# Multiplying the reciprocal norm in where the first stage modulates its rows, straight from PSUM

## The chip, the core and the metric

One core of a Trainium2 chip runs the whole program. The metric is device time in microseconds of one execution; for the kernel before, three runs gave 1878.0, 1878.12 and 1881.57 us, so the median is 1878.12 us.

## What is computed

Two layers of a diffusion backbone run over 512 latent tokens and 256 context tokens, with 1024 channels. The change touches only the start of the first layer, where every token is normalized, scaled and shifted before the input projections:

```python
def rmsnorm(x, w):
    y = xf * lax.rsqrt(jnp.mean(xf * xf, axis=-1, keepdims=True) + EPS)
    return y * w
def modulate(h, shift, scale):
    return h * (1 + scale) + shift
mod   = split(c_act  @ mod_w[layer] + mod_b[layer], 6)
mod_c = split(cc_act @ mod_w[layer] + mod_b[layer], 6)
hx = modulate(rmsnorm(x, norm_mix_w[layer]), mod[0], mod[1])
hc = modulate(rmsnorm(h_ctx, norm_mix_w[layer]), mod_c[0], mod_c[1])
```

The projections `hx @ ab_w_in` and `hc @ ab_w_in` follow, then the DeltaNet and attention heads, the output projection, the feed-forward network, and a second layer with other heads.

## The kernel before, in words

Activations lie with the channels on the partitions: `xt` is 8 blocks of 128 channels by 768 tokens (512 latent, 256 context). Every large product is done in three passes: each operand is split into a high part in a rounded format (`hi`, `wh`) and a low part with the rest (`lo`, `wl`), and TensorE adds `wh*hi`, `wh*lo` and `wl*hi`. A split is one ScalarE copy (L247 for weights, L405 for activations) and one subtraction (L197, by VectorE, or by GpSimd for every other activation block).

The first stage is in `body`, L1692 to L1712. `norm_stats` (L368) sums the squares of the 8 blocks, gets the reciprocal norm of each token, and lets TensorE spread it over all partitions into two PSUM tiles with the tag `mm`: one for the 512 latent tokens, one for the 256 context tokens. Then L1701 to L1703 multiply `xt` by them in place, with two VectorE instructions for each of the 8 blocks, 16 in all.

The loop at L1706 runs four times. Step i calls `mod` (L312), which loads 2 MB of modulation weights in two transfers, multiplies on TensorE (64 short matmuls), copies the result out of PSUM (L328), transposes it (L194) and adds the bias (`modc`). `scale_shift` makes the scales (`samix`). `hx0` (L394) then modulates the channel blocks 2i and 2i+1: two VectorE `tensor_scalar` instructions for each block (L403, recorded as L214), which write a tile `hxt` (three buffers), then the split (L405, L406). At i = 1 `dn_begin` (L690) takes the first two weights of the convolution projections, and for each of them two PSUM tiles of the tag `mm`; `dn_part` (L693) then adds channel blocks 0 and 1 at step 1, 2 and 3 at step 2, and 4 and 5 at step 3, for both weights: 6 matmuls of 384 columns for each block and weight. Blocks 6 and 7 are added in `dn_conv` (L697). Its ScalarE copies (L712) empty the PSUM tiles, and the third weight follows.

The tag `mm` has four PSUM buffers (L1695). In the kernel before, the two norm tiles have been read for the last time when the 16 multiplications are done, so that all four are there for the two begun weights. The queues run in an order fixed when the program is built: a planner places each engine's instructions by the program's order, by when their inputs are ready in its model, and by when a buffer is free; an instruction whose tile has no free buffer yet is placed behind the release. All transfers of this stage are issued in order on SP's queue (L221).

The stage for the later norms, `hx` (L408), already has the form that the change brings in: VectorE multiplies a block by its scale and by the norm from PSUM in one instruction (L420), and ScalarE adds the shift (L424).

Of the kernel before, what the change touches and what calls it, by code (L numbers as in the profile page):

```python
# [13 lines left out]
AF = mybir.ActivationFunctionType  # L14
ALU = mybir.AluOpType
# [6 lines left out]
KD = D // P  # L22
NL = 512
NC = 256
NT = NL + NC
# [123 lines left out]
class Kern:  # L149
# [241 lines left out]
            K.mm(o, rs[:, i:i + 1].broadcast_to([P, P]), K.ident)  # L391
        return pl, pc

    def hx0(self, xt, act, sa, sb, d0):  # L394
        K = self
        if d0 % 4 == 0:
            for a in act:
                x = K.t(K.bp, (P, 4, NT), "hx", F32R, bufs=4)
                a.extend(x[:, d] for d in range(4))
        for d in range(2):  # L400
            t = K.t(K.sx, (P, NT), "hxt", bufs=3)
            for c, g in ((slice(0, NL), 0), (slice(NL, NT), 1)):
                K.ts(t[:, c], xt[:, d0 + d, c], sa[:, d, g:g + 1], sb[:, d, g:g + 1])  # L403
            hi, lo = act[0][d0 + d], act[1][d0 + d]
            K.A.copy(out=hi, in_=t)  # L405
            K.sub(lo, t, hi, K.G if d % 2 else K.V)  # L406

# [1271 lines left out]
def body(ctx, tc, I, out, dbg=None, stop=None):  # L1679
    K = Kern(ctx, tc, I, out, dbg)  # L1680
    K.setup()
    hD = K.t(K.dp, [2, 2, P, 2, 2, 512], "hD")
    hsD = K.t(K.dp, [2, 4, P, 2, 512], "hsD")
    sg, sp = ExitStack(), ExitStack()
    K.pg = K.pool(sg, "dn_g", side="right")
    mp0 = K.pool(sp, "mp0", side="right")
    half = lambda w, ns: [(w[n][i], (4, 256)) for n in ns for i in range(2)]
    outp = lambda w, n: [(w[n][dp], (2, 4, P)) for dp in range(4)]
    K.stream([(I["abf"][n], (KD, P)) for n in (4, 5, 6, 7, 0, 1, 2, 3)] + [(I["abg"], (KD, P))]
             + [(I["abf"][n], (KD, P)) for n in (8, 9, 10, 11)] + half(I["abt"], (4, 5, 2, 3, 0, 1))  # L1690
             + outp(I["abo"], 1) + outp(I["abo"], 0))
    with ExitStack() as s:  # L1692
        with ExitStack() as s2:
            K.mp, K.mpn = K.pool(s2, "mps"), 6
            K.psum(mm=4, wk=4)  # L1695
            K.sp = K.sx = K.pool(s2, "sp0", side="right")
            xt = K.t(K.bp, (P, KD, NT), "x", bufs=1)
            for d in range(0, KD, 2):
                K.dma(xt[:, d:d + 2], I["xall"][:, d:d + 2])
            st = K.norm_stats(xt)  # L1700
            for d in range(KD):  # L1701
                for c, r in ((slice(0, NL), st[0]), (slice(NL, NT), st[1][:, :NC])):
                    K.mul(xt[:, d, c], xt[:, d, c], r)  # L1703
            act = ([], [])
            begun = []
            for i in range(4):  # L1706
                K.mod(i)
                K.hx0(xt, act, *K.scale_shift(0, "mix", 2 * i, 2), 2 * i)
                if i == 1:
                    begun = [K.dn_begin() for _ in range(2)]  # L1710
                for b in begun:
                    K.dn_part(b, act, range(2 * i - 2, 2 * i))  # L1712
        K.mp, K.mpn = mp0, 1
        pf = K.pool(s, "hyf0")
        K.tasks["hy"] = [K.hy_time(pf, hsD)]
        K.tasks["mod"] = [K.mod_gen(range(4, 10))]
        conv = K.l0_conv(act, sg, sp, begun)
        K.drain("hy")
    od, x1D, oh = K.l0_mixers(act, conv)
    if stop == "mix0":  # L1720
        for k in range(KD):
            h = K.t(K.cp, (P, NT), "dbh", bufs=1)
            o = od if k < 4 else oh
            K.tt(h, o[0][:, k % 4], o[1][:, k % 4], ALU.add)
            K.dma(dbg["o"][k], h)
        return
    xt = K.t(K.bp, (P, KD, NT), "x", bufs=1)
    for d in range(KD):
        K.dma(xt[:, d], x1D[:, d])
    K.out_half(None, 0, od, xt, None, NT)  # L1730
    saf, sbf = K.scale_shift(0, "ffn")
    with ExitStack() as s:
        K.sp = K.sx = K.pool(s, "sp1", side="right")
        pf = [K.pool(s, "hyf1a"), K.pool(s, "hyf1b", side="right")]
        act = K.hx(xt, K.norm_stats(xt), saf, sbf)
        K.hy_freq(*pf, 0, hsD, hD)
    with ExitStack() as s:
        K.hp, mp = K.pool(s, "hp"), K.pool(s, "mp1", side="right")
        K.tasks["mod"] = [K.mod_rows(mp, [(0, n, True) for n in range(40, 48)] + [(1, n, n < 16) for n in range(48)])]
        K.ffn(0, act, xt, 2)  # L1740
        K.drain("mod")
    if stop == "l0":
        K.dma(dbg["x"], xt)
        return
    sa1, sb1 = K.scale_shift(1, "mix")
    xD = K.t(K.dp, [P, KD, NL], "xD")
    x2D = K.t(K.dp, [P, KD, NL], "x2D")
    with ExitStack() as s:
        K.sp, pa, K.sx, pf = (K.pool(s, n, side="right") for n in ("sp2", "hyf2a", "sx2", "hyf2b"))
        act = K.hx(xt, K.norm_stats(xt), sa1, sb1)  # L1750
        K.dma(xD, xt[:, :, :NL])
        K.hy_freq(pa, pf, 1, hsD, hD)
    K.stream([(I["hyf"][n], (KD, P)) for n in range(12)] + half(I["rett"], (2, 3, 4, 5, 0, 1, 6, 7))
             + outp(I["cdo"], 1) + outp(I["cdo"], 0)[:2])
    od, oh = K.l1_mixers(act, hD, xD, x2D)
    if stop == "mix1":
        for k in range(KD):
            h = K.t(K.cp, (P, NL), "dbh", bufs=1)
            o = od if k < 4 else oh
            K.tt(h, o[0][:, k % 4, :NL], o[1][:, k % 4, :NL], ALU.add)  # L1760
            K.dma(dbg["o"][k], h)
        return
    xt = K.t(K.bp, (P, KD, NL), "x", bufs=1)
    for d in range(KD):
        K.dma(xt[:, d], x2D[:, d])
    with ExitStack() as s:
        K.sp = K.sx = K.pool(s, "sp3", side="right")
        K.hp = K.pool(s, "hp1")
        act, rest = K.out_norm(K.pool(s, "wo", side="right"), od, xt, *K.scale_shift(1, "ffn", nr=1))
        K.ffn(1, act, xt, 1, lambda d: K.dma(out[:, d], xt[:, d]), rest)  # L1770
# [15 lines left out]
```

## Time and profile before

| | us |
|---|---|
| median of three runs | 1878.12 |
| the profiled execution | 1882.48 |
| its span, first to last instruction | 1880.7 |
| what lies around the span | 1.8 |

The profile is of one execution, and its rows are of that one; it took 4.4 us longer than the median. Times in the rows count from the span's start. PE is TensorE, and PEld its loading of weights; DVE is VectorE, ACT ScalarE, POOL GpSimd, SP the queue that issues transfers. A group of instructions has its count, its busy time, the mean of one in ns, and the idle time of its engine just before it with what ended that idle time. In a timeline, like instructions that follow one another are put together in one row. The line number is that of the helper that recorded an instruction (L190 for every matmul, L197 for two-tensor operations, L210 for `scalar_tensor_tensor`, L214 for `tensor_scalar`, L218 for activations).

### The profile page before, as it was taken

What the parts mean: (1) busy time and instruction counts of PE and PEld (TensorE: products, weight loads), DVE (VectorE), ACT (ScalarE), POOL (GpSimd) and SP (SyncE); (2) the same over time, 40 slices, a digit from 0 to 9 for tenths busy, and PEclk for the clock granted to TensorE, in tenths of its full rate; (3) what the DMA queues carried; (4) which work ended last, traced back from release to release, by engine and by line L of the source; (5) the groups of instructions that cost most, each with busy time, mean ns of one, the idle gap of its engine ahead of it and who ended that gap; (6) DMA issues with size and microseconds to landing.
All of it is one profiled execution on the core that took longest, in us unless ns stands there. A gap on an engine that the chain in (4) does not pass through costs nothing.

```text
span 1880.7 us, 28131 instructions
## 1 busy us (share of the span) xinstructions
PE 1803.7 (96%) x11311; PEld 1642.2 (87%) x11311; DVE 1024.8 (54%) x2053; ACT 604.3 (32%) x1215; POOL 87.3 (5%) x94
## 2 busy tenths in 40 slices
PE   4999999999899999899999999999999999999999
PEld 4988899988697999899999998687998888888887
DVE  5785696558747886642222234768645663333333
ACT  2543534235615322111211222522443442222221
POOL 0011000100002000000000000100003100000000
PEclk9998999779999999999999999999999999999999
DMA  8343366355372666652222123432433523333332
GB/s 328 111 152 122 121 204 189 99 163 182 127 261 99 192 193 221 213 180 68 57 60 76 55 60 122 157 96 94 126 134 102 180 79 97 94 101 90 101 97 94
DMA packets 105790, 248.92 MB, mean 132 GB/s; under 512 B 26809, under 2 KB 41577, under 8 KB 101948
## 3 DMA queue, kind: packets, MB, share of 16 engines
q1 hardware_dynamic: 105660, 247.12, 41.3%
q8 instruction: 89, 1.46, 0.3%
q14 instruction: 41, 0.34, 0.1%
HBM read 210.09 MB, written 37.00 MB: 131 GB/s over the span
## 4 chain that ended last, share of the span: by engine, by line
PE 67%; DVE 10%; DMA 6%; issue 2%; ACT 2%; DVEq 0%; POOLq 0%; ACTq 0%; SPq 0%
PE mm L190 45%; PE wk L190 20%; DMA wm<-in_modt_dram 4%; DVE wl L197 2%; DVE wj L210 1%; PE sa L190 1%; PE wk L194 1%; DVE hxt L210 1%; ACT wh L247 1%; PE sa L194 1%; DVE hx L197 1%; DMA rkD<-rr 1%; DVE uc L210 0%; DVE ivt L197 0%; DMA rvt<-rvD 0%
## 5 line engine op out<-in xcount | busy, mean ns | idle before, releaser
L190 PE MATMUL mm<-hx,wh 128*128 128x384 f32 (+2 forms) x2496 | 713.4, 355 | 7.4 <-ACT hx L405 4.3
L190 PEld LDWEIGHTS mm<-hx,wh 128*128 128x128 f32 x2496 | 457.6, 190 | 50.9 <-ACT hx L405 4.5
L247 ACT CAST wh<-wr 128x1024 fp32r<-128x1024 f32 (+1 forms) x205 | 212.7, 1038 | 804.7 <-PE mm L190 414.2
L190 PE MATMUL mm<-hx,wl 128*128 128x384 f32 (+2 forms) x1248 | 416.3, 355 | 5.0 <-DVE wl L197 4.9
L197 DVE TENSOR_TENSOR wl<-wr,wh 128x1024 fp32r<-128x1024 f32 (+1 forms) x205 | 247.7, 1209 | 252.4 <-ACT wh L247 248.9
L190 PEld LDWEIGHTS mm<-hx,wl 128*128 128x128 f32 x1248 | 233.5, 189 | 29.5 <-DVE wl L197 7.6
L190 PE MATMUL wk<-hx,wh 128*128 128x384 f32 x704 | 235.8, 335 | 0.0
L190 PE MATMUL mm<-wh,hx 128*128 128x256 f32 x1216 | 232.7, 290 | 1.7 <-DVE sv L960 1.1
L190 PEld LDWEIGHTS mm<-wh,hx 128*128 128x128 f32 x1216 | 194.5, 195 | 4.5 <-issue 1.7
L190 PE MATMUL mm<-wl,hx 128*128 128x256 f32 x608 | 175.8, 290 | 0.0
L210 DVE SCALAR_TENSOR_TENSOR x<-mm,modc,x 128x384 f32<-128x384 f32 (+3 forms) x88 | 50.5, 590 | 181.9 <-PE mm L190 181.9
L190 PEld LDWEIGHTS wk<-hx,wh 128*128 128x128 f32 x704 | 132.7, 188 | 0.2 <-issue 0.2
L190 PE MATMUL mm<-hhi,wl 128*128 128x384 f32 (+1 forms) x352 | 127.6, 362 | 3.4 <-DVE wl L197 3.4
L190 PE MATMUL mm<-hlo,wh 128*128 128x384 f32 (+1 forms) x352 | 127.3, 362 | 0.0
L190 PE MATMUL mm<-hhi,wh 128*128 128x384 f32 (+1 forms) x352 | 127.3, 362 | 0.0
L210 DVE SCALAR_TENSOR_TENSOR wj<-wm,cb 128x1024 bf16<-128x1024 f32 x80 | 97.9, 1223 | 53.3 <-DMA wm<-in_modt_dram 49.3
L190 PEld LDWEIGHTS mm<-wl,hx 128*128 128x128 f32 x608 | 118.6, 195 | 1.0 <-issue 0.6
L190 PE MATMUL wk<-hx,wl 128*128 128x384 f32 x352 | 118.0, 335 | 0.0
L197 DVE TENSOR_TENSOR hf<-hf,mm 128x384 f32<-128x384 f32 (+1 forms) x44 | 27.3, 620 | 147.5 <-PE mm L190 147.3
L190 PEld LDWEIGHTS mm<-hhi,wl 128*128 128x128 f32 x352 | 66.1, 188 | 11.3 <-DVE wl L197 4.4
L190 PEld LDWEIGHTS mm<-hhi,wh 128*128 128x128 f32 x352 | 66.1, 188 | 6.9
L190 PEld LDWEIGHTS mm<-hlo,wh 128*128 128x128 f32 x352 | 66.1, 188 | 6.8
(371 smaller groups left out, 2295.5 us busy)
## 6 DMA issues: line engine op xcount, KB each, us to landing
wr<-in_ffi_dram SPq DMA_DIRECT2D x88, 512.0 KB
wm<-in_modt_dram SPq DMA_DIRECT2D x56, 512.0 KB
wm<-in_modw_dram SPq DMA_DIRECT2D x20, 1024.0 KB
wr<-in_ffo_dram SPq DMA_DIRECT2D x32, 448.0 KB
wr<-in_ffo_dram SPq DMA_DIRECT2D x16, 512.0 KB
wr<-in_rett_dram SPq DMA_DIRECT2D x16, 512.0 KB
wr<-in_abf_dram SPq DMA_DIRECT2D x12, 512.0 KB
wr<-in_abt_dram SPq DMA_DIRECT2D x12, 512.0 KB
```

What stands on the lines that cost most here:

```text
L190: self.T.matmul(out=out, lhsT=l, rhs=r, start=start, stop=stop, skip_group_check=True)
L194: self.T.transpose(out, in_, self.ident[:n, :n])
L197: (eng or self.V).tensor_tensor(out=out, in0=a, in1=b, op=op)
L210: self.V.scalar_tensor_tensor(out=out, in0=a, scalar=s, in1=b, op0=op0, op1=op1, **kw)
L247: self.A.copy(out=hi, in_=raw)
```

## The change

The pass of 16 multiplications is taken out. In `hx0`, `tensor_scalar` (times scale, plus shift) becomes `scalar_tensor_tensor` (times scale, times the norm read from PSUM) on VectorE, and the shift is added in place by a ScalarE `Identity` activation with a bias, ahead of the copy to `hi`. The norm's two PSUM tiles are now read for the last time in the last call of `hx0`.

```diff
-    def hx0(self, xt, act, sa, sb, d0):
+    def hx0(self, xt, st, act, sa, sb, d0):
...
         for d in range(2):
             t = K.t(K.sx, (P, NT), "hxt", bufs=3)
+            hi, lo = act[0][d0 + d], act[1][d0 + d]
             for c, g in ((slice(0, NL), 0), (slice(NL, NT), 1)):
-                K.ts(t[:, c], xt[:, d0 + d, c], sa[:, d, g:g + 1], sb[:, d, g:g + 1])
-            hi, lo = act[0][d0 + d], act[1][d0 + d]
+                K.stt(t[:, c], xt[:, d0 + d, c], sa[:, d, g:g + 1], st[g][:, :c.stop - c.start], ALU.mult, ALU.mult)
+                K.act(t[:, c], t[:, c], AF.Identity, bias=sb[:, d, g:g + 1])
             K.A.copy(out=hi, in_=t)
             K.sub(lo, t, hi, K.G if d % 2 else K.V)
...
             st = K.norm_stats(xt)
-            for d in range(KD):
-                for c, r in ((slice(0, NL), st[0]), (slice(NL, NT), st[1][:, :NC])):
-                    K.mul(xt[:, d, c], xt[:, d, c], r)
             act = ([], [])
...
-                K.hx0(xt, act, *K.scale_shift(0, "mix", 2 * i, 2), 2 * i)
+                K.hx0(xt, st, act, *K.scale_shift(0, "mix", 2 * i, 2), 2 * i)
```

## Rows read from the trace of the kernel before

**Rows 1.** The page, part 4: the chain that ended last, by engine and by line

```profile
PE 67%; DVE 10%; DMA 6%; issue 2%; ACT 2%; DVEq 0%; POOLq 0%; ACTq 0%; SPq 0%
PE mm L190 45%; PE wk L190 20%; DMA wm<-in_modt_dram 4%; DVE wl L197 2%; DVE wj L210 1%; PE sa L190 1%; PE wk L194 1%; DVE hxt L210 1%; ACT wh L247 1%; PE sa L194 1%; DVE hx L197 1%; DMA rkD<-rr 1%; DVE uc L210 0%; DVE ivt L197 0%; DMA rvt<-rvD 0%
```

**Rows 2.** Groups by form, 20 to 62 us: form, count, busy us, mean ns, idle before

```profile
L405 ACT CAST hx<-hxt 128x768 fp32r<-128x768 f32 x8 | 6.5, 837 | 10.6 <-DVE hxt L214 10.6
...
L197 DVE TENSOR_TENSOR x<-x,mm 128x512 f32<-128x512 f32 x8 | 5.5, 681 | 2.2 <-PE mm L190 2.2
L214 DVE TENSOR_SCALAR hxt<-x,samix,modc 128x512 f32<-128x512 f32 x8 | 4.3, 541 | 0.2
L247 ACT CAST wh<-wr 128x1024 fp32r<-128x1024 f32 x4 | 4.2, 1050 | 1.3 <-PE mm L190 1.3
L197 DVE TENSOR_TENSOR hx<-hxt,hx 128x768 fp32r<-128x768 f32 x4 | 3.8, 958 | 0.4
...
L197 DVE TENSOR_TENSOR x<-x,mm 128x256 f32<-128x256 f32 x8 | 3.3, 416 | 0.2 <-PE mm L190 0.2
L214 DVE TENSOR_SCALAR hxt<-x,samix,modc 128x256 f32<-128x256 f32 x8 | 3.2, 406 | 0.0
```

**Rows 3.** Groups by form, 590 to 612 us: the same modulation in a later stage

```profile
L210 DVE SCALAR_TENSOR_TENSOR hxt<-x,saffn,mm 128x512 f32<-128x512 f32 x8 | 5.9, 740 | 1.2 <-PE mm L190 1.2
...
L210 DVE SCALAR_TENSOR_TENSOR hxt<-x,saffn,mm 128x256 f32<-128x256 f32 x8 | 3.8, 471 | 0.0
...
L218 ACT ACTIVATE hxt<-hxt,modc 128x512 f32<-128x512 f32 x4 | 2.9, 715 | 0.0
...
L218 ACT ACTIVATE hxt<-hxt,modc 128x256 f32<-128x256 f32 x4 | 2.0, 511 | 2.5 <-DVE hxt L210 2.5
```

**Rows 4.** Timeline of all engines, first 45 us: start, length, instruction, idle before

```profile
27.77 0.69 DVE L197 TENSOR_TENSOR x<-x,mm 128x512 f32<-128x512 f32 x1 [2.16 <-PE mm L190]
...
28.63 6.93 DVE L197 TENSOR_TENSOR x<-x,mm 128x256 f32<-128x256 f32 x15 [0.17 <-PE mm L190]
...
30.53 0.33 PE L194 MATMUL wk<-cst,modsb 128*128 128x128 f32 x1 [0.40 <-ACT modsb L328]
...
32.81 0.27 ACT L328 COPY modsb<-wk 128x128 f32<-128x128 f32 x1 [2.33 <-PE wk L190]
...
35.93 1.65 DVE L214 TENSOR_SCALAR hxt<-x,samix,modc 128x512 f32<-128x512 f32 x4
36.83 0.83 ACT L405 CAST hx<-hxt 128x768 fp32r<-128x768 f32 x1 [2.81 <-DVE hxt L214]
...
37.71 2.99 PE L190 MATMUL mm<-hx,wh 128*128 128x384 f32 x6 [4.26 <-ACT hx L405]
...
39.18 0.43 SPq L221 DMA_DIRECT2D wm<-in_modw_dram  x1
```

**Rows 5.** Timeline of PE alone, 25 to 64 us

```profile
44.63 1.96 PE L190 MATMUL wk<-wm,cpad 128*32 128x128 f32 x64
...
55.18 0.85 PE L190 MATMUL mm<-hx,wh 128*128 128x384 f32 x4
...
57.26 0.85 PE L190 MATMUL mm<-hx,wh 128*128 128x384 f32 x4
...
61.40 0.51 PE L190 MATMUL mm<-hx,wl 128*128 128x384 f32 x2
```

**Rows 6.** Timeline of all engines from 45 us on

```profile
47.14 0.27 PE L194 MATMUL wk<-cst,modsb 128*128 128x128 f32 x1
...
47.99 1.65 DVE L214 TENSOR_SCALAR hxt<-x,samix,modc 128x512 f32<-128x512 f32 x4
...
54.35 1.65 DVE L214 TENSOR_SCALAR hxt<-x,samix,modc 128x512 f32<-128x512 f32 x4
```

**Rows 7.** Windows of 1 us: busy PE, PEld, DVE, ACT, POOL; granted clock; DMA

```profile
35.00:36.00 1.00, 0.00 (x0) 0.00 (x0) 0.97 (x7) 0.00 (x0) 0.00 (x0) 0.80 1.00 418
...
41.00:42.00 1.00, 1.00 (x5) 1.00 (x4) 1.00 (x2) 0.00 (x0) 0.33 (x1) 0.50 1.09 434
```

## The prediction

> **What bounds the kernel now.** I read the chain that ended last first, because it says which engine pays for a microsecond lost. TensorE's matmuls hold 67% of it, VectorE 10%, and the two matmul groups that lead it (tags mm and wk) 65% by themselves [rows 1]. So a step of the first stage is worth what it brings forward TensorE's work, and nothing more. Next the groups by form of the first stage: the pass to be removed is 8 multiplications of 512 columns and 8 of 256, 5.5 and 3.3 us busy, against 4.3 and 3.2 us for the 16 modulations and 6.5 us for the 8 copies to `hi` [rows 2]. Then the timeline, for where the pass stands. It runs from 27.77 to 35.6 us with VectorE never free; the first modulation follows at 35.93, the first `hi` is ready at 37.66, and TensorE's first projection matmul starts at 37.71, after 4.26 us idle for which the row names that copy [rows 4]. So at the start the pass is on the chain.
>
> What TensorE does next sets how much of that is real. Twelve matmuls take from 55.18 to 57.26 us, 0.174 us each, with no gap [rows 5]. The two begun weights need 2 x 8 blocks x 6 = 96 of them, 16.7 us, and the two remaining modulation blocks 2.0 + 0.27 us each, 4.5 in all [rows 5, 6]. The last of this work starts at 61.40 and ends two matmuls later, at 61.75 [rows 5]. From 37.71 that is 24.0 us for 21.2 us of work: TensorE was nearly saturated, and most of the 2.8 us lies at the front, where the 24 matmuls of blocks 0 and 1 took until 44.63, 6.9 us for 4.2 us of work. There the granted clock had fallen to half, 1.2 GHz, after the idle time (0.80 mean in the microsecond from 35, 0.50 in the one from 41) [rows 4, 5, 7]. The mark to compare with is this 61.75.
>
> **The change part by part.** *The removed pass.* VectorE loses 8.8 us busy. What can start instead needs `modc`, whose first transposition ends at 30.86 us [rows 4]; from the end of a transposition to the first modulation takes 0.58 us (47.41 to 47.99) [rows 6]. So the first modulation starts at 31.4, not 35.93.
>
> *The new VectorE form.* The same instruction from PSUM stands in a later stage: 740 ns for 512 columns and 471 for 256 [rows 3]. Sixteen of them make 9.7 us against 7.5 [rows 2], so VectorE saves 6.6 us net. The Trainium skill (VectorE: DVE Perf Modes, section "The perf-mode tier table") would speak against this: it gives an fp32 operation with one tensor twice the rate of one with two, 1227 against 2293 ns for 2048 elements. By that ratio an estimate for the 16 would be 14.0 us and the net saving 2.3; the trace shows 740 against 541 ns and the measurement decides.
>
> *The added ScalarE work.* Sixteen activations of 715 and 511 ns, 9.8 us, on an engine that had 6.5 us of copies and 2.1 us of weight copies here [rows 2, 3]. No instruction is moved to POOL, and no transfer is added. The new activations write `hxt` in place between the modulation and the split, so both halves of the split wait for them. A block now costs ScalarE 0.72 + 0.51 + 0.84 = 2.06 us, and ScalarE is the feed's pace. First `hi`: 31.4 + 0.74 + 0.72 + 0.51 + 0.84 = 34.2 us; with one modulation copy (0.27) and one weight copy (1.05) between them, which need the same engine before TensorE can start [rows 2, 4], 35.5. I take 35.5, since ScalarE issued both close to this point before. That is 2.2 us earlier than 37.66.
>
> *The tiles held longer.* This is the part that speaks against the change. The norm's two PSUM tiles are two of the four `mm` buffers, and their last reader is now the modulation of block 7. The first begun weight gets the other two; the second must wait. Its 36 matmuls for blocks 0 to 5 move behind that reader, and behind them stand the 24 of blocks 6 and 7 for both weights: 60 x 0.174 = 10.4 us that cannot begin before it. So the end is at least the last modulation's end plus 10.4, and level with before at 61.75 - 10.4 = 51.3. In the trace of before that modulation ends at 54.35 + 1.65 = 56.0 [rows 6].
>
> *When the last modulation ends.* With three `hxt` buffers, block 7 needs the buffer of block 4, free after its `lo`. ScalarE reaches `hi` of block 4 at 35.5 + 1.05 (second weight) + 0.27 + 4 x 2.06 = 45.1; `lo` adds 0.96, the modulation itself 1.21: 47.2 us is the early end. The late end is the old pace of the steps, earlier by the 2.2 us alone: 56.0 - 2.2 = 53.8. Between them stand the hand-overs to blocks 2 and 3 of the modulation. One, from the end of its matmuls at 46.59 to the first modulation at 47.99, costs 1.4 us [rows 5, 6]. The first is covered by the three buffers; I charge one: 48.6. Block 3's second transfer, issued at 39.18 [rows 4], stands on SP's queue behind a weight whose buffer is freed by a `wl` subtraction. That subtraction stood behind the removed pass, so the transfer should come earlier rather than later; I cost it at nothing, and if it came 2 us later, so would everything in this sum.
>
> *The sum.* TensorE ends this block at 48.6 + 10.4 = 59.0 against 61.75: **2.7 us earlier**. All that follows hangs on it and should shift alike. The profiled execution took 1882.48 us, its span 1880.7, so its successor would take 1879.8. That execution stands 4.4 us above the median, so from 1878.12 I forecast **1875.4**. Since 0.2%, about what a measurement of this kernel can tell from no change, is 3.8 us, this is a gain that would count as none.
>
> **The rivals.** *The feed is as quick as it can be.* If neither hand-over shows, the last modulation ends at 47.2 and the block at 57.6, 4.1 us earlier: 1874.0. The outer bound is TensorE alone, started at 34.2 and never idle: 34.2 + 21.2 = 55.4, 6.3 us earlier, 1871.8. For it: both early modulation blocks' matmuls were done by 33.5 and TensorE has room for the other two while only one weight can be fed. Against it: ScalarE's 2.06 us a block leaves it no slack.
>
> *Nothing moves.* The steps run in series again, because the planner keeps each modulation block behind the previous step's matmuls, as at 44.63 [rows 5]; the last modulation ends near 51.3 and the held tiles take back the head start: 1878.1. The same number comes out if a later wait on a transfer swallows the shift (transfers hold 6% of the chain) [rows 1].
>
> *The held tiles decide, slower.* The place is TensorE's queue at the second weight's first matmul. Past 51.3, each microsecond of the last modulation is one of the end. At the old pace, 53.8, the end is 64.2, 2.5 us later. With half of its matmuls out of reach TensorE then idles before the release, and if the clock falls as it did at 35, the front's loss of 2.7 us is paid once more: 5.2 us later, 1883.3. For it: two of four buffers are taken for the whole stage, and ScalarE gets more than twice its work. The Trainium skill (Perfetto Trace Analysis, section "Optimization Strategy") says that a gap repeating on the engine that should be saturated can mean there isn't enough PSUM for the next tile. By that rule this rival is the likely one; the trace of before has no such gap here, and none there can show it.
>
> That the change doesn't do what it says is hardly possible: the pass is deleted.
>
> **How the numbers follow.** Forecast 0.32; quick feed 0.28; nothing moves 0.16; slower 0.24, since the order that the planner makes of the rest is seen in no row. Only the quick feed passes 3.8 us on one side and only the held tiles, with the clock, on the other: faster 0.28, same 0.48, slower 0.24. The range goes from TensorE's bound, 1871.8, to the slower rival's, 1883.3.
>
> **What would show it.** Right: no L197 pass at 27.77; the first L210 modulation near 31.4 and the first projection matmul near 35.5; the second weight's matmuls in one run of 36 behind the last modulation, which ends near 48.6; blocks 6 and 7 done near 59.0; a granted clock of 1.00 over most of 36 to 42 us. Wrong: the last modulation after 51.3, a long idle time of TensorE just before it, a clock of 0.50 there, or a later stage in which the two traces lose or win more than this shift.

## The result: slower by 0.51%, outside the range

The changed kernel takes 1887.62 us (median of 8 runs, 1881.67 to 1890.34) beside 1878.06 us for the kernel before (8 runs of the same set): 9.6 us more, a ratio of 1.0051 with an interval of 1.0035 to 1.0067. The prediction was 1875.4 us, with 1883.3 as the upper end.

The page of the changed kernel's profiled execution (1890.15 us), parts 1 and 4: span, busy time by engine, and the chain that ended last by engine.

```profile
span 1888.3 us, 28125 instructions
...
PE 1805.5 (96%) x11311; PEld 1642.7 (87%) x11311; DVE 1018.0 (54%) x2037; ACT 611.2 (32%) x1231; POOL 87.2 (5%) x94
...
PE 75%; DVE 13%; DMA 6%; issue 3%; ACT 3%; SPq 0%; POOL 0%; DVEq 0%; POOLq 0%; ACTq 0%
```

VectorE is busy 6.8 us less than before (1024.8 there), ScalarE 6.9 us more (604.3), and the span is 7.6 us longer. So the work went where the diff sends it (the 16 activations sum to 9.7 us; neighbouring rows of ScalarE overlap by some 0.1 us), and the loss is not busy time of these two engines: it is on the chain, which TensorE still leads as in [rows 1]. The groups by form of the changed kernel, 30 to 66 us (count, busy us, mean ns, idle before), confirm the prices of the new instructions:

```profile
L210 DVE SCALAR_TENSOR_TENSOR hxt<-x,samix,mm 128x512 f32<-128x512 f32 x8 | 6.0, 745 | 0.7 <-DVE samix L210 0.5
L218 ACT ACTIVATE hxt<-hxt,modc 128x512 f32<-128x512 f32 x8 | 5.8, 720 | 8.0 <-DVE hxt L210 8.0
...
L218 ACT ACTIVATE hxt<-hxt,modc 128x256 f32<-128x256 f32 x8 | 3.9, 494 | 0.0
...
L210 DVE SCALAR_TENSOR_TENSOR hxt<-x,samix,mm 128x256 f32<-128x256 f32 x8 | 3.8, 475 | 0.0
```

All four are within 4% of the rows of the later stage that they were taken from [rows 3].

**Where the time went.** The same landmarks in both traces tell it, after minus before. The first PSUM copy of the second begun weight moves from 62.56 to 73.22 us (+10.7), that of the third weight from 71.17 to 81.67 (+10.5). The last of these rows in the kernel before is this; in the change it ends the second timeline below.

```profile
71.17 0.47 ACT L712 COPY xp<-mm 128x384 f32<-128x384 f32 x1
```

So the whole loss exists by 72 us. From there on for ScalarE, VectorE and SP, and from 91 us on for TensorE's matmuls, the two traces have the same instructions in the same order, and the difference is carried along: +5.3 at a transfer of the first layer's scan (403.7 to 409.0), +9.1 at the feed-forward norm's modulation (591.8 to 600.9), +10.8 at the second layer's last first-stage modulation (1188.6 to 1199.4), +7.6 at the end. It wanders with the granted clock of later stretches: from 120 to 183 us it is 0.86 before and 0.92 after, 8.8 and 5.0 us lost (one minus the clock, times 63), and from 480 to 540 us 0.94 and 0.86, 3.6 and 8.4 us lost.

Now the first stage itself. The timeline of all engines of the changed kernel, 31 to 43 us (start, length, instruction, idle before):

```profile
31.68 1.95 PE L190 MATMUL wk<-wm,cpad 128*32 128x128 f32 x64
...
32.26 2.19 DVE L210 SCALAR_TENSOR_TENSOR hxt<-x,samix,mm 128x512 f32<-128x512 f32 x4
33.04 1.12 ACT L218 ACTIVATE hxt<-hxt,modc 128x512 f32<-128x512 f32 x2 [1.67 <-DVE hxt L210]
34.19 0.83 ACT L406 CAST hx<-hxt 128x768 fp32r<-128x768 f32 x1
...
36.82 0.26 ACT L328 COPY modsb<-wk 128x128 f32<-128x128 f32 x1
36.98 1.05 ACT L247 CAST wh<-wr 128x1024 fp32r<-128x1024 f32 x1
...
37.13 0.33 PE L194 MATMUL wk<-cst,modsb 128*128 128x128 f32 x1 [3.49 <-ACT modsb L328]
...
38.08 1.65 PE L190 MATMUL mm<-hx,wh 128*128 128x384 f32 x4 [0.62 <-ACT wh L247]
38.85 2.19 DVE L210 SCALAR_TENSOR_TENSOR hxt<-x,samix,mm 128x512 f32<-128x512 f32 x4
...
40.96 2.35 DVE L197 TENSOR_TENSOR wl<-wr,wh 128x1024 fp32r<-128x1024 f32 x2
...
42.23 1.01 PE L190 MATMUL mm<-hx,wl 128*128 128x384 f32 x2 [2.51 <-DVE wl L197]
```

The pass is gone, and the first modulation starts at 32.26 in place of 35.93 [rows 4]. But the 64 matmuls of modulation block 1, which end at 33.64, find their copy out of PSUM (L328) behind four new activations and two copies in ScalarE's fixed order. It runs at 36.82, where before it ran at 32.81 [rows 4], and TensorE stands idle for 3.49 us. The `wh` copy of the first weight stands behind the same work, so the first projection matmul starts at 38.08: before, 37.71. The head start of 3.7 us is spent before TensorE sees any of it. Then `wl` stands behind step 1's modulations on VectorE and TensorE waits 2.51 us more. Those modulations are themselves 0.9 us late by something else: the instruction that makes their scales, 0.16 us in the other steps, takes 1.06 us from 37.76 on and ends with GpSimd's subtraction for channel block 1 (36.99 to 38.80).

The same timeline, 45 to 82 us:

```profile
45.09 1.94 PE L190 MATMUL wk<-wm,cpad 128*32 128x128 f32 x32
...
48.77 1.08 PE L190 MATMUL wk<-wm,cpad 128*32 128x128 f32 x32
...
50.41 0.27 PE L194 MATMUL wk<-cst,modsb 128*128 128x128 f32 x1
...
50.97 1.08 PE L190 MATMUL wk<-wm,cpad 128*32 128x128 f32 x32
...
51.23 2.19 DVE L210 SCALAR_TENSOR_TENSOR hxt<-x,samix,mm 128x512 f32<-128x512 f32 x4
...
54.05 0.62 PE L190 MATMUL mm<-hx,wh 128*128 128x384 f32 x2 [2.01 <-ACT hx L406]
...
55.66 1.94 PE L190 MATMUL wk<-wm,cpad 128*32 128x128 f32 x32
...
58.66 0.41 PE L194 MATMUL wk<-cst,modsb 128*128 128x128 f32 x1
...
60.02 2.19 DVE L210 SCALAR_TENSOR_TENSOR hxt<-x,samix,mm 128x512 f32<-128x512 f32 x4 [0.49 <-DVE samix L210]
...
61.88 0.61 PE L190 MATMUL mm<-hx,wh 128*128 128x384 f32 x2 [0.89 <-DVE hxt L210]
...
72.41 0.85 PE L190 MATMUL mm<-hx,wh 128*128 128x384 f32 x4
...
73.22 0.91 ACT L713 COPY xp<-mm 128x384 f32<-128x384 f32 x3
...
81.67 0.47 ACT L713 COPY xp<-mm 128x384 f32<-128x384 f32 x1
```

In [rows 5] the 64 matmuls of modulation block 2 are one run from 44.63 to 46.59. Here they are two halves, at 45.09 and 48.77, with matmuls of the first weight between them; block 3's halves start at 50.97 and 55.66, 4.7 us apart, with a wait of 2.01 us for step 2's `hi` between them. Only the first weight may be fed, so its matmuls, which wait for each step's split, stand among the matmuls that the next step needs. The transposition of block 3 runs at 58.66, before at 53.50, and the last modulations at 60.02 to 62.21, before 54.35 to 56.0 [rows 6]. Only then come the second weight's matmuls, with `[<-DVE hxt]` as the releaser: the freed PSUM tile. The 60 matmuls behind that release run from 61.88 to 72.41.

Windows of the changed kernel (us; busy time of PE, PEld, DVE, ACT and POOL with counts; granted clock, DMA share, GB/s):

```profile
46.00:47.00 1.00, 1.00 (x21) 0.59 (x13) 0.00 (x0) 0.00 (x0) 0.21 (x1) 0.50 0.06 16
...
54.00:55.00 1.00, 0.62 (x2) 0.30 (x2) 0.96 (x1) 1.00 (x2) 0.00 (x0) 0.84 0.20 50
55.00:56.00 1.00, 0.95 (x9) 0.61 (x13) 0.00 (x0) 0.86 (x2) 0.04 (x1) 0.50 0.54 186
...
61.00:62.00 1.00, 0.12 (x1) 0.12 (x2) 1.00 (x3) 0.97 (x3) 0.00 (x0) 0.75 0.97 377
...
```

The clock is at 1.2 GHz from 37.6 to 47.8 us, behind the wait of 3.49 us, and again from 54.7 to 61.5, behind the wait of 2.01 us (a mean of 0.84 in a window is half clock for 0.32 us of it, one of 0.75 for 0.5 us; the windows from 37 and 47 us have 0.80 and 0.58). Before it was low once, from 35.6 to 42.4 us, with the 0.80 and the 0.50 of [rows 7] among its windows. It can also be seen in the timeline: a half of a modulation block takes 1.94 us at 45.09 and 1.08 at 48.77.

From 38.08 to 72.41 are 34.3 us for the same 21.2 us of work that before took 24.0. Of the 13.1 us lost, 5.8 are the waits named in brackets (2.51 + 2.01 + 0.89, and 0.37 in a row not shown). The low clock, over 9.8 us of the first stretch and 6.8 of the second less the waits in them, costs about 6.6: (9.8 - 2.5 + 6.8 - 0.9) / 2.

### The profile page after: what moved, and what is told of

Same layout as the page of the kernel before. It is cut to its first block, busy times and chain, and to the rows that moved or that the text cites. A ratio compares the mean times of both kernels' runs of the same rounds, so it can differ in the third digit from the quotient of the medians.

```text
span 1888.3 us, 28125 instructions
## 1 busy us (share of the span) xinstructions
PE 1805.5 (96%) x11311; PEld 1642.7 (87%) x11311; DVE 1018.0 (54%) x2037; ACT 611.2 (32%) x1231; POOL 87.2 (5%) x94
## 4 chain that ended last, share of the span: by engine, by line
PE 75%; DVE 13%; DMA 6%; issue 3%; ACT 3%; SPq 0%; POOL 0%; DVEq 0%; POOLq 0%; ACTq 0%
PE mm L190 50%; PE wk L190 22%; DMA wm<-in_modt_dram 3%; DVE wl L197 2%; DVE wj L210 1%; PE wk L194 1%; PE sa L190 1%; DVE hxt L210 1%; DVE ac L210 1%; DVE hx L197 1%; PE sa L194 1%; ACT wh L247 1%; DMA rkD<-rr 1%; DVE ivt L197 0%; DVE hx L210 0%
```

## The experiments

Two causes stood against each other. **The held tiles**: the norm's PSUM tiles are read until the last step, the second weight waits, and the order around it falls apart. **The activations**: ScalarE's longer work for a block delays the small copies in front of TensorE. A third was that a later stage adds something of its own.

The mark used below is the first PSUM copy of the third weight in each profile, the first point behind all of this work: 71.17 us before, 81.67 after. Second profiles of the same kernels gave 70.76 and 80.32, so it holds to about 1.5 us. Each ratio is against the runs of the kernel before in the same set, whose medians lay between 1876.57 and 1879.57 us.

| kernel | mark, us | against 71.17 | time, us | ratio and interval |
|---|---|---|---|---|
| the change | 81.67 | +10.5 | 1887.62 | 1.0051 [1.0035, 1.0067] |
| the change, again | 80.32 | +9.2 | 1887.13 | 1.0046 [1.0031, 1.0061] |
| before, as a candidate | 70.76 | -0.4 | 1877.13 | 0.9987 [0.9970, 1.0004] |
| hold alone (e2) | 80.27 | +9.1 | 1885.87 | 1.0052 [1.0032, 1.0071] |
| activations alone (e7) | 77.29 | +6.1 | 1885.37 | 1.0034 [1.0017, 1.0051] |
| change without hold (e1) | 74.72 | +3.6 | 1885.55 | 1.0042 [1.0024, 1.0059] |
| the same, again (f3) | 74.66 | +3.5 | 1884.15 | 1.0040 [1.0023, 1.0057] |
| change, `hi` by the activation (e4) | 77.47 | +6.3 | 1882.69 | 1.0027 [1.0014, 1.0040] |
| both, no hold and `hi` (e5) | 73.86 | +2.7 | 1881.27 | 1.0015 [0.9996, 1.0034] |
| modulation first (e3) | 81.35 | +10.2 | 1884.10 | 1.0042 [1.0027, 1.0056] |
| modulation copy on VectorE (e10) | 76.84 | +5.7 | 1881.29 | 1.0023 [1.0003, 1.0043] |
| e5 and that (e11) | 73.99 | +2.8 | 1883.39 | 1.0027 [1.0012, 1.0043] |
| blocks in pairs (e17) | 81.00 | +9.8 | 1887.06 | 1.0033 [1.0013, 1.0052] |
| e1 in pairs (e23) | 76.48 | +5.3 | 1883.80 | 1.0032 [1.0016, 1.0048] |
| e5, pairs, early weights (e20) | 73.35 | +2.2 | 1879.31 | 1.0002 [0.9985, 1.0018] |
| before, pairs, early weights (e22) | 73.27 | +2.1 | 1880.61 | 1.0000 [0.9985, 1.0015] |

### Take the hold out of the change (e1)

The norm is copied to SBUF once, by two VectorE copies, and the modulation reads the copy:

```diff
-            st = K.norm_stats(xt)
+            ps = K.norm_stats(xt)
+            st = [K.t(K.sx, (P, n), f"nsb{g}") for g, n in ((0, NL), (1, NC))]
+            for o, p in zip(st, ps):
+                K.V.tensor_copy(out=o, in_=p[:, :o.shape[1]])
```

> The change, but the norm is copied from its two PSUM tiles into SBUF by two VectorE copies as soon as it is spread, and the modulation reads the copy; the PSUM tiles are free before the loop. Theory 1 (the held PSUM tiles): the second begun weight runs beside the first again, its matmuls for blocks 0 to 5 no longer come in one run behind the last modulation, and blocks 6 and 7 are done near 60 to 62 us instead of 72.4; the time is 1875 to 1881 us, about that of the kernel before. Theory 2 (the 9.8 us more of ScalarE work in the feed): the modulations stay as late as in the change, the last one ends after 57 us, and the time stays above 1884 us.

The mark falls by 7.0 us, from 81.67 to 74.72; in the second pair of profiles by 5.7 (80.32 to 74.66). The modulation blocks are whole again. What is left is the wait for block 1's copy, and a step 2 that comes 2.1 us later than before [rows 6]. The timeline of this kernel:

```profile
35.87 0.47 PE L194 MATMUL wk<-cst,modsb 128*128 128x128 f32 x1 [3.40 <-ACT modsb L328]
...
46.70 1.95 PE L190 MATMUL wk<-wm,cpad 128*32 128x128 f32 x64
...
50.04 2.21 DVE L210 SCALAR_TENSOR_TENSOR hxt<-x,samix,nsb 128x512 f32<-128x512 f32 x4
...
74.72 0.48 ACT L713 COPY xp<-mm 128x384 f32<-128x384 f32 x1
```

So in the changed kernel the hold is worth 5.7 to 7.0 us of the first stage. Part of the difference between the two pairs is where block 0's transposition starts (31.43 in the change and 30.26 in e1, 30.31 and 31.27 in the repeats); counted from there the two pairs give 5.8 and 6.6. The time does not follow in full: it falls by about 3 us (1887.13 to 1884.15 in one set), and its ratio still is 1.0040 to 1.0042. More on that at the end of this section.

### Add the hold alone to the kernel before (e2)

The pass stays. Two one-column products read the norm's tiles once more, behind the high part of block 7; nothing uses what they write. So the tiles are held until 57.5, 1.2 us past the last modulation's end (56.3).

```diff
                 if i == 1:
                     begun = [K.dn_begin() for _ in range(2)]
+                if i == 3:
+                    for g in range(2):
+                        K.tt(K.t(K.sx, (P, 1), f"held{g}"), st[g][:, 0:1], act[0][7][:, 0:1].bitcast(F32), ALU.mult)
```

> The kernel before with its pass and its tensor_scalar, and two VectorE instructions of one column each that read the norm's PSUM tiles once more when the last block's high part is ready; nothing else is changed. Theory 1 (held tiles): the second weight waits for them, which are free near 57 us, and 60 matmuls of 0.174 us follow: blocks 6 and 7 are done near 66 to 68 us against 61.75, and the time is 1882 to 1886 us (4 to 7 us over the kernel before), more if the matmuls of the modulation blocks are placed behind waiting ones. Theory 2 (ScalarE): no ScalarE work is added, so the time is that of before, 1876 to 1880 us.

Two instructions of 0.1 us each cost 9.1 us at the mark and a ratio of 1.0052, as much as the whole change. The timeline of this kernel:

```profile
42.36 1.08 PE L190 MATMUL wk<-wm,cpad 128*32 128x128 f32 x32
...
44.81 1.08 PE L190 MATMUL wk<-wm,cpad 128*32 128x128 f32 x32
...
56.45 2.96 PE L190 MATMUL mm<-hx,wh 128*128 128x384 f32 x7 [2.36 <-ACT hx L405]
57.30 0.22 DVE L197 TENSOR_TENSOR held<-mm,hx 128x1 f32<-128x1 f32 x2
...
59.84 1.48 PE L190 MATMUL mm<-hx,wh 128*128 128x384 f32 x4
...
63.24 0.85 PE L190 MATMUL mm<-hx,wh 128*128 128x384 f32 x4
...
70.81 0.91 ACT L712 COPY xp<-mm 128x384 f32<-128x384 f32 x3
```

The halves are here too (block 2's are shown; block 3's start at 47.71 and 52.16), with the old modulation and the old ScalarE work: the hold is enough to split the modulation blocks. The release at 57.5 is 4.7 us earlier than in the change (62.2), yet the second weight's copy comes only 2.4 earlier (70.81), because the matmuls behind it start at half clock: four in 1.48 us at 59.84, in 0.85 at 63.24.

### Add the activations alone to the kernel before (e7)

The pass stays and no tile is held. Only the shift moves from `tensor_scalar` to 16 activations:

```diff
-                K.ts(t[:, c], xt[:, d0 + d, c], sa[:, d, g:g + 1], sb[:, d, g:g + 1])
+                K.ts(t[:, c], xt[:, d0 + d, c], sa[:, d, g:g + 1], None, ALU.mult)
+                K.act(t[:, c], t[:, c], AF.Identity, bias=sb[:, d, g:g + 1])
```

> The kernel before with its pass, which frees the PSUM tiles before the loop; only the shift is moved from VectorE's modulation to the 16 ScalarE activations of the change. Theory 2 (ScalarE: the activations stand in its queue ahead of the modulation blocks' copies, and in each block's feed): the modulations come later than before, blocks 6 and 7 are done at 66 to 70 us instead of 61.75, and the time is 1882 to 1887 us. Theory 1 alone (held tiles): no tile is held, blocks 6 and 7 are done by 63 us, and the time is 1875 to 1880 us.

The mark moves by 6.1 us and the ratio is 1.0034. Its timeline:

```profile
34.22 0.33 PE L194 MATMUL wk<-cst,modsb 128*128 128x128 f32 x1 [0.39 <-ACT modsb L328]
...
38.97 2.10 PE L190 MATMUL mm<-hx,wh 128*128 128x384 f32 x4 [4.42 <-ACT hx L406]
...
51.16 0.27 PE L194 MATMUL wk<-cst,modsb 128*128 128x128 f32 x1
...
77.29 0.48 ACT L713 COPY xp<-mm 128x384 f32<-128x384 f32 x1
```

With the pass kept, block 1's copy isn't delayed (0.39 us, as in [rows 4]); the feed is. Block 2's matmuls are cut up here as well, into pieces of 2 to 22 between 41.64 and 50.6 us, and it is transposed at 51.16, where before it was at 47.14 [rows 6]. So here a feed that is late cuts a block up without any hold; block 3 stays whole (54.49). From e7 to e1 the pass goes (two copies of the norm, 1.1 us, come, and the modulation takes the dearer form with the norm in it), and the mark falls by 2.6 us: that is what the removed pass gives in the presence of the rest, less those two. So the first stage adds up as activations +6.1, pass -2.6, hold +7.0: +10.5. The last two terms are differences of neighbouring rows of the table, so the sum must come out; by itself, on the kernel before, the hold costs 9.1, so the terms depend on one another.

### Make ScalarE's part smaller (e4, e5)

The activation writes `hi` itself, and VectorE makes `lo` in one instruction for each of the two column ranges. Eight ScalarE copies and the GpSimd subtractions go.

```diff
-                K.act(t[:, c], t[:, c], AF.Identity, bias=sb[:, d, g:g + 1])
-            K.A.copy(out=hi, in_=t)
-            K.sub(lo, t, hi, K.G if d % 2 else K.V)
+                K.act(hi[:, c], t[:, c], AF.Identity, bias=sb[:, d, g:g + 1])
+                K.stt(lo[:, c], t[:, c], sb[:, d, g:g + 1], hi[:, c].bitcast(F32), ALU.add, ALU.subtract)
```

> The change, but the activation that adds the shift writes the high part itself and VectorE makes the low part in one instruction, so the 8 ScalarE copies of 768 columns (6.7 us) go and the 4 GpSimd subtractions move to VectorE; the PSUM tiles are still held. Theory 2 (ScalarE): the last modulation comes 4 us or more earlier than in the change, and the time falls to 1880 to 1884 us. Theory 1 with theory 3 (held tiles, released late because of TensorE's order): the last modulation moves by less than 3 us, and the time stays at 1884 to 1889 us.

> The change with both suspected costs taken away: the norm is copied from PSUM into SBUF by two VectorE copies before the loop, and the activation that adds the shift writes the high part itself (no 8 copies of 768 columns on ScalarE, the low part by VectorE). If the loss is the sum of the held tiles and of ScalarE's queue, blocks 6 and 7 are done at 58 to 62 us (before: 61.75, the change: 72.4) and the time is 1873 to 1879 us. If something else loses the time (the granted clock, VectorE, which gets 16 instructions for the low parts), they are done after 64 us and the time stays above 1881 us.

On the change alone (e4) it gives back 4.2 us of the mark, and 1.0027. Not all of that is ScalarE's: with no subtraction on GpSimd, step 1's scale instruction takes 0.16 us in place of 1.06. Together with the copy of e1 (e5) the mark is +2.7 and the interval of the ratio, 0.9996 to 1.0034, includes 1. With both causes weakened most of the loss is gone; but there is no gain either.

### Change the order of the modulation blocks (e3, e17, e23)

If the blocks' matmuls stand among those of the first weight, calling them earlier should help. In e3 all four `mod` calls stand ahead of the loop; in e17 blocks 0 and 1 are made and scaled together, and then 2 and 3; e23 is e17 with the copy of e1.

```diff
             for i in range(4):
-                K.mod(i)
-                K.hx0(xt, st, act, *K.scale_shift(0, "mix", 2 * i, 2), 2 * i)
+                if i % 2 == 0:
+                    K.mod(i)
+                    K.mod(i + 1)
+                    sa, sb = K.scale_shift(0, "mix", 2 * i, 4)
+                K.hx0(xt, st, act, *(x[:, 2 * (i % 2):2 * (i % 2) + 2] for x in (sa, sb)), 2 * i)
```

> The change, with the four modulation blocks written ahead of the loop instead of one in each step; the norm's PSUM tiles are still held to the last modulation. Theory 3 (the release is late because the matmuls of modulation blocks 2 and 3 are queued behind matmuls of the first weight that wait for the step before): the last modulation ends near 50 to 54 us instead of 62.2, blocks 6 and 7 are done near 61 to 65 us, and the time is 1877 to 1881 us. Theory 2 (ScalarE sets the pace of the feed): the last modulation still ends after 57 us and the time stays above 1883 us.

> The change with only the order of the modulation blocks altered: blocks 0 and 1 are finished, and one set of scales made from both, before the first modulation, then blocks 2 and 3 before the fifth; so a modulation block's copy on ScalarE can't stand behind the activations of the block before. The norm's PSUM tiles are still held. If the late release is made by that queue (theory 3 with theory 2), the last modulation ends at 50 to 55 us instead of 62.2, blocks 6 and 7 are done at 61 to 66 us instead of 72.4, and the time is 1877 to 1882 us. If the held tiles cost about 6 us whatever the order, or if the 9.8 us of activations alone set the pace, blocks 6 and 7 are done after 68 us and the time stays above 1884 us.

> Both together: modulation blocks in pairs as above, and the norm copied from PSUM into SBUF before the loop. If the two causes add, blocks 6 and 7 are done at 56 to 61 us (before: 61.75) and the time is 1872 to 1878 us; if the activations' own 9.8 us set the pace of the feed, they are done after 62 us and the time is 1878 us or more.

None of the three wins back what was hoped for: marks of +10.2, +9.8 and +5.3 us. The timeline of e3 shows why:

```profile
36.46 0.47 PE L194 MATMUL wk<-cst,modsb 128*128 128x128 f32 x1 [3.49 <-ACT modsb L328]
...
43.06 0.47 PE L194 MATMUL wk<-cst,modsb 128*128 128x128 f32 x1 [2.99 <-ACT modsb L328]
...
49.72 0.48 PE L194 MATMUL wk<-cst,modsb 128*128 128x128 f32 x1 [2.93 <-ACT modsb L328]
50.67 1.65 PE L190 MATMUL mm<-hx,wh 128*128 128x384 f32 x4 [0.47 <-ACT wh L247]
```

The small copy of each block is placed behind the previous step's activations, so each block costs 6.6 us in series, and the first weight waits until 50.67. The last modulation does start earlier (56.4, after 61.7 in the change), but that is no gain, as the 96 matmuls of the two weights had only begun at 50.67. In e17 block 1 is copied at once (34.17), but TensorE waits 4.13 us until 38.62, as it did before until 37.71, and 3.38 us until 54.75, both times for `hi`.

### Take the small copy off ScalarE (e10, e11)

```diff
-            K.A.copy(out=sb, in_=ps[:, :P])
+            K.V.tensor_copy(out=sb, in_=ps[:, :P])
```

> The change with one thing moved: the copy of a modulation block's result out of PSUM goes from ScalarE to VectorE (in all ten blocks), so that it no longer stands behind the new activations; the tiles are still held. If ScalarE's queue delays the modulation blocks, block 1 is transposed near 34 us instead of 37.13, the last modulation ends 3 to 6 us earlier than 62.2, and the time is 1880 to 1885 us. If TensorE's order alone makes the release late, the last modulation stays within 2 us of 62.2 and the time at 1885 to 1890 us.

> The kernel with the copied norm and the high part written by the activation, and besides the copy of the modulation blocks on VectorE. If ScalarE's queue still holds the modulation blocks back there, blocks 6 and 7 are done another 1 to 3 us earlier than without it and the time is 1871 to 1877 us; if not, the two are level within 2 us.

Block 1's copy was to be free of the queue. It is not: in e10 it stands behind VectorE's modulations, and its row reads

```profile
36.19 0.33 PE L194 MATMUL wk<-cst,modsb 128*128 128x128 f32 x1 [2.63 <-DVE modsb L328]
```

so 0.9 us is won there. But the later blocks come earlier as well (47.68 and 54.33, after 50.41 and 58.66), the last modulation starts at 56.9, and of 10.5 us 4.8 are given back, at 1.0023. On top of e5 it gives nothing (e11).

### Two versions meant to beat both (e20, e22)

e20 is e5 with the pairs and with the first two weights written ahead of the loop, their low parts on GpSimd; e22 puts the same order (the pairs, the early weights, GpSimd) into the kernel before, without the change.

```diff
             begun = []
+            first = [K.dn_begin() for _ in range(2)]
...
                 if i == 1:
-                    begun = [K.dn_begin() for _ in range(2)]
+                    begun = first
```

> A version meant to beat both: norm copied to SBUF, high part written by the activation, modulation blocks in pairs, and the first two weights written ahead of the loop, with their low parts by GpSimd, so that they are split before the first activation is ready. TensorE's first projection matmul near 35 to 36 us, blocks 6 and 7 done at 55 to 59 us, 1871 to 1877 us. If what is left is TensorE's own 21.2 us of work and a halved clock in front, they are done at 59 to 62 us and the time is that of before.

> The kernel before, pass and tensor_scalar kept, with the same early weights and paired modulation blocks: what the reordering is worth without the change. If the pass on VectorE still sets the first projection matmul (37.7 us before), it starts at 36.5 to 38 us, blocks 6 and 7 are done at 58 to 61 us and the time is 1874 to 1878 us.

Both are level with the kernel before, 1.0002 and 1.0000. Neither beats it. Their order has a price of its own: the two weights' transfers are issued ahead of the modulation's (in e22 from 5.87 us, the modulation's from 7.66; before, from 9.88 and 5.28), and block 0's transposition starts at 31.95 and 32.63, after 30.53 before.

### Repeats, and what stays open (f1 to f3)

> The kernel before once more, against itself. If the clock lost in the later stretches varies from run to run and is not tied to a kernel, this profile loses another amount between 480 and 560 us than the 3.2 us of the first one (5 to 10 us have been seen in other kernels), and the ratio is 1.000 within 0.002. If it is tied to the kernel, the loss there is 3 to 4 us again.

> The change once more. Its second PSUM copies start near 73 us again (the first stage doesn't vary by more than 1.5 us), and the time is 1883 to 1889 us, 0.3 to 0.6% over the kernel before; the loss between 480 and 560 us is another than 8.8 us if it varies from run to run.

> The change with the norm copied to SBUF, once more. If its earlier 1885.55 us came from a low granted clock in later stretches by chance, it comes out 3 to 5 us over the kernel before now (ratio 1.0015 to 1.003), as its first stage has it (3 us later); if the held tiles cost nothing in the end, it comes out level with the change, 1.0045 or more.

The kernel before against itself gives 0.9987, an interval with 1 in it; the change repeats, 1.0046, and so does e1, 1.0040. This leaves a question. Over the 16 rows of the table the time, less the median before in its set, follows the mark (correlation 0.75), but e1 and f3 take 8.4 and 7.6 us more than the kernel before in their sets, 4 to 5 us above the difference of their marks. Their runs have a mean granted clock of 0.9749 and 0.9752, those of the kernel before 0.9783 and 0.9784 in the same two sets. The stretch in which it falls isn't settled: both of their profiles lose 10.2 us of clock between 480 and 540 us, but so does e22, which is level. Why the kernel with the copied norm draws a lower clock later is open.

## Why the prediction was wrong

**The removed pass, the new form, the added activations:** right. The first modulation was put at 31.4 and is at 32.26; VectorE's net saving at 6.6 and is 6.8 us; the VectorE form at 740 and 471 ns and is 745 and 475; a block on ScalarE at 2.06 us and is 1.89 (33.04 to 34.93). The ratio of the 512-column form to the old one is 745 / 541 = 1.38, and not the 1.87 (2293 / 1227) that the figures of the Trainium skill (VectorE: DVE Perf Modes, section "The perf-mode tier table") give.

**First projection matmul, 35.5:** it is 38.08. The sum had one modulation copy and one weight copy between block 0's instructions. The planner put both behind both channel blocks of step 0: the activations of the second block and its `hi` come first. In the change that is the first wait of the loss, 3.49 us. The activations cost TensorE time in another place as well: in e7 they come to +6.1 us by themselves, with that copy on time and a wait of 4.42 us for `hi`.

**The tiles held longer:** the rule held to 0.2 us. The end is the last modulation's end plus 10.4 us: 62.2 + 10.4 = 72.6, measured 72.41. The second weight's 36 matmuls do stand behind that release.

**"When the last modulation ends":** this is the step that failed. It said 48.6, between 47.2 and 53.8; measured 62.2, 8.4 us beyond the late end. The hand-overs to modulation blocks 2 and 3 were charged 1.4 us, once. In the changed kernel VectorE waits 6.54 and 4.12 us for their transpositions:

```profile
50.72 0.23 DVE L197 TENSOR_TENSOR modc<-wk,colv 128x4 f32<-128x4 f32 x2 [6.54 <-PE wk L194]
...
59.11 0.23 DVE L197 TENSOR_TENSOR modc<-wk,colv 128x4 f32<-128x4 f32 x2 [4.12 <-PE wk L194]
```

In e1, where no tile is held, the same two rows are

```profile
49.52 0.23 DVE L197 TENSOR_TENSOR modc<-wk,colv 128x4 f32<-128x4 f32 x2 [6.58 <-PE wk L194]
...
55.90 0.23 DVE L197 TENSOR_TENSOR modc<-wk,colv 128x4 f32<-128x4 f32 x2 [1.59 <-PE wk L194]
```

So the first of these waits is there without the hold, and most of the second comes with it. Two sentences of the prediction were wrong.
- "The first is covered by the three buffers; I charge one." The first hand-over, from block 1's matmuls to step 1's modulations, isn't covered: 33.64 to 38.85 is 5.2 us. It needs the copy at L328, and I counted ScalarE's time for a block but not what stands behind it in ScalarE's order. Of the 5.2 us, 0.9 are the scale instruction that ends with GpSimd's subtraction, which I hadn't seen either, though in the kernel before it takes 1.79 us (39.56 to 41.35).
- "The late end is the old pace of the steps, earlier by the 2.2 us alone." The old pace is 6.5, 5.6 and 6.4 us from step to step. In the change the steps are 6.6, 12.4 and 8.8 us apart (in its repeat 6.6, 12.2 and 8.8), in e1 6.5, 12.5 and 6.6 (in its repeat 6.5, 11.3 and 6.6), and in e2, with the hold alone, 6.5, 5.6 and 7.4. So the long second step comes with the activations: in e1 the 24 matmuls of blocks 0 and 1, which stand ahead of modulation block 2, take from 36.82 to 46.70, 9.9 us in place of 6.9, with a wait of 2.02 us for the second `wh` copy and the clock at 0.50 in the windows from 36 to 45 us. The hold makes the third step 2.2 us longer. The last modulation of e1 ends at 58.9, so 5.0 of the 8.4 us beyond the late end are there without any hold. I priced the hold as 36 matmuls behind the release and the activations as ScalarE's pace, and took it to be zero what either does to the place of the modulation blocks in TensorE's order.

**The rivals.** "The held tiles decide, slower" had the place and the rule, at 0.24, and priced it 2.5 to 5.2 us; measured 10.7 us at that point. Its upper price allowed one more fall of the clock of 2.7 us; the clock was in fact at half for 17.0 us in all (10.2 and 6.8). The Trainium skill (Perfetto Trace Analysis, section "Optimization Strategy") says that a gap repeating on the engine that should be saturated can mean too little SBUF or PSUM for the next tile. The trace agrees in part: e2, whose edit only releases two PSUM tiles later, has TensorE waiting 8.8 us for splits between 30 and 62 us, where the kernel before waits 4.3. But its gaps are of 0.3 to 4.0 us, and the rows name the splits, not a PSUM tile.

"Nothing moves" had the steps in series, as they came out, but took it for granted that the head start would pay for it; in fact they were further apart than before. That block 3's second transfer waits on SP's queue was a misreading of [rows 4]: the first stage's eight transfers are all issued by 30.5 us, and the one at 39.18 is the next stage's.

**The range** ended at 1883.3 because the last modulation's late end was tied to the old pace. A late end with step 2 and 3 each waiting for the step before in full would have been outside of it.

## What to carry to other kernels

Before an operand is read straight from PSUM, count the buffers of its tag: a pass that looks redundant may be what frees two of four, and here two 0.1 us reads at the end of the stage cost as much as the whole change. Where the order of the queues is made by a planner, a tile held longer, or work added to a feed, moves other tiles' work too, so the pace of the trace before can't be carried over as a bound. And when work is added to an engine off the bound, look for the small copy that TensorE waits for, and for what will stand in front of it.

## What was not expected of the hardware

- Reading the norm from SBUF is no quicker than from PSUM: in the kernel with the copy, the 512-column form has a mean of 748 ns over 8 and the 256-column form 478, against 745 and 475 from PSUM. What the copy buys in this kernel is the freed tile alone.
- Some VectorE instructions take longer while GpSimd subtracts. The one that makes the scales, with its operands in SBUF, takes 0.16 us, but 1.06 in the change and 1.79 in the kernel before, where it starts during a subtraction, and ends within 0.02 us of it both times. Of two 512-column modulations that start during a subtraction, the one with the norm in SBUF takes 2.32 us (e23, from 40.92), the one with the norm in PSUM 0.74 (e17, from 41.29). That last comparison is one instance of each.
- One program's time follows the mean granted clock of the execution: 25 runs of the kernel before in one set go from 1871.36 us at 0.982 to 1883.96 us at 0.974; a straight line through the 25 gives some 1.3 us for 0.001 (correlation -0.91). The stretches are not the same each time: between 480 and 540 us, one profile of the kernel before has a clock of 0.94, the next 0.86.
- A wait of 2.01 us was followed by half clock for 6.8 us (54.7 to 61.5), while TensorE was busy 6.07 of the 7 us from 55 to 62. Half of the 6.8 us, less the 0.9 us of waits in them, is 3.0 us: here the clock behind the wait cost more than the wait.
